# Low halves of the projections' weights and their sums of squares on VectorE instead of GpSimd

## The chip, the core and the metric

The program runs on one core of one Trainium2 chip. A core has five engines that work side by side, each from its own list, in order: TensorE (PE in the profile; its weight loads are PEld), VectorE (DVE), ScalarE (ACT), GpSimd (POOL) and SyncE (SP), which here issues nearly all DMA transfers. An instruction starts when it is at the head of its engine's list and the semaphores that it waits for are set. The metric is the time of one execution on the device in microseconds; the figure for a kernel is the median of its runs.

## The reference

Two layers over 1024 latent tokens and 256 context tokens of width 1024, in float32. Cut to what matters here:

```python
for l in range(2):
    mod = silu(c) @ w_mod[l] + b_mod[l]          # six shifts, scales and gates; the same for c_ctx
    h = rmsnorm(x, g_norm1[l]) * (1 + sc1) + sh1  # the same for the context
    pf, mq, mk, mv, mo, mg, cq, ckv, kr = split(h @ w_in[l])
    y_f = real(fft2(pf))
    q, k = silu(conv5([mq, mk]))                  # depthwise, 5 taps
    y_m = mlstm_both_directions(q, k, mv, gates(mg)) * sigmoid(mo)
    y_a = attention(rmsnorm(cq) @ w_uq, rmsnorm(ckv) @ w_ukv, kr)
    x = x + ga1 * (concat(y_f, y_m, y_a) @ w_out[l])
    x = x + ga2 * (square(relu(modulate(rmsnorm(x, g_norm2[l])) @ w_up[l])) @ w_down[l])
return rmsnorm(x, g_final)
```

## The kernel before

**Numbers in two halves.** TensorE multiplies float32r operands. To keep the accuracy of float32, `split` writes every operand as a high half (ScalarE, a copy in float32r, line 147) and a low half (source minus high half, line 148), and `mm3` forms a product from three matmuls: high by high, high by low, low by high (lines 138, 143, 144 among others). `split` gives the low half to GpSimd where its caller names no engine.

**Tiles.** Tokens go in three blocks (`BLK`): two of 512 latent tokens and one of 256 context tokens. Features lie on the partitions, 128 at a time, so one elementwise instruction is mostly 128x512.

**Weights of the projections.** `wunit` fetches a piece of 128x512 (SyncE, line 167) into `wf`, a ring of three buffers, and splits it into `wr`, a ring of ten. `unit` calls it four times for one unit of the input projection; the output projection calls it too, through `wtile`. The first two units of layer 0 land in parts of the input's own buffers instead of `wf` (`wr<-x` in the profile), and some at the start of layer 1 in `r`. The low half stands on VectorE for the odd ones of the first eight calls, on GpSimd for all others. `wq` and `wkv`, the weights of the attention's second projections, are fetched and split in the same manner beside the gates' arithmetic (line 644).

**Norms.** A sum of squares over the features is collected tile by tile: ScalarE squares, a second engine adds (`accum_ss`, line 267, for the low-rank norms and the output projection; lines 348 to 351 at the start; `put`, line 1426, at the end of the MLP, which stays as it is). `rstd_bcast` sums over the partitions on TensorE, computes the inverse root by three Newton rounds, on GpSimd (lines 180 to 183) or VectorE (185 to 187), and spreads it by TensorE again (line 201). At the start, block 0 takes the GpSimd form, and GpSimd then multiplies the eight tiles by it (line 359). The low-rank norms take the GpSimd form in layer 1 only (`LNE`).

**Modulation.** `modulate` (blocks 1 and 2 in layer 0) writes the halves of eight tiles; for odd `k` through `split`. `mod0` (block 0) has its own choice of engines and stays.

**Around the convolution.** For each of six tiles of mq and mk, TensorE projects, ScalarE copies into `rb` (line 673), VectorE does five taps (675, 677), ScalarE a tanh, VectorE the closing product (679). Between these rows VectorE does the products of weights and `c` that give the modulation of later stages (line 235, weight tiles `gt` and `wf` fetched by SyncE at line 232), the norms, and the mLSTM gates (lines 580 to 635), whose vectors take a turn through DRAM (lines 593 to 599: `dA` and `dB` out, `A` and `B` back).

**What sets the order.** The code is written stage by stage with priorities. The tile framework then sets each engine's list by an estimated timeline of the whole program, so that an instruction given to another engine also changes the order of rows around it, on all engines. The lists themselves are fixed when the program runs.

Of the kernel before, what the change touches and what calls it, by code (L numbers as in the profile page):

```python
# [9 lines left out]
ALU = mybir.AluOpType  # L10
# [53 lines left out]
def build(tc, A, out, dbg=None):  # L64
# [9 lines left out]
    def T(pool, shape, dt=F32, tag=None, **kw):  # L74
        if tag in alias:
            tag, kw = alias[tag], {}
            if isinstance(tag, tuple):
                pool, tag = tag
        assert kw == seen.setdefault((id(pool), tag), kw) or not kw, tag
        kw = seen[(id(pool), tag)]  # L80
        return pool.tile(list(shape), dt, tag=tag, name=nm(tag), **kw)
# [24 lines left out]
    V, S, G, PE = nc.vector, nc.scalar, nc.gpsimd, nc.tensor  # L106

    def f32(ap):
        return ap.bitcast(F32)
# [36 lines left out]
    def split(dst, src, hi=None, lo=None):  # L146
        (hi or S).activation(dst[0], src, AF.Copy) if (hi is None or hi is S) else hi.tensor_copy(dst[0], src)  # L147
        (lo or G).tensor_tensor(dst[1], src, f32(dst[0]), ALU.subtract)  # L148
# [11 lines left out]

    NRING = 10

    wcnt = [0, 9]

    def wunit(src, f=None):
        f = T(ring, [128, 512], tag="wf", bufs=3) if f is None else f
        nc.sync.dma_start(f, src)
        r = T(ring, [128, 2, 512], F32R, tag="wr", bufs=NRING)
        wcnt[0] += 1
        split((r[:, 0], r[:, 1]), f, lo=V if wcnt[0] < wcnt[1] and wcnt[0] % 2 else G)  # L170
        return r

    def rstd_small(y, v, n, pool, rows=128, eng=None):
# [87 lines left out]
    def accum_ss(ss, x, j, pool, n, eng=None):  # L261
        if j == 0:
            S.activation(ss[:, :n], x, AF.Square)
        else:
            sq = T(pool, [128, 512], tag="sq")
            S.activation(sq[:, :n], x, AF.Square)
            (eng or G).tensor_tensor(ss[:, :n], ss[:, :n], sq[:, :n], ALU.add)

    def modulate(l, i, b, xt, ss, h, pool, psp, tag):
        n, w = BLK[b][1], BLK[b][2]  # L270
        R = rstd_bcast(ss, n, D, pool, psp, tag)
        for k in range(8):
            t = T(pool, [128, 512], tag="md_t")[:, :n]
            V.scalar_tensor_tensor(t, xt[:, k, :], Gm[l][i][:, w, k:k + 1], R[:, :n], ALU.mult, ALU.mult)
            sh = modT[l][:, w, 24 * i + k:24 * i + k + 1]
            if k % 2 == 0:
                S.activation(h[:, 0, k, :], t, AF.Identity, bias=sh)
                V.scalar_tensor_tensor(h[:, 1, k, :], t, sh, f32(h[:, 0, k, :]), ALU.add, ALU.subtract)
            else:
                S.activation(t, t, AF.Identity, bias=sh)  # L280
                split((h[:, 0, k, :], h[:, 1, k, :]), t)

    big = {}

# [33 lines left out]
    ss = [T(xp, [128, BLK[b][1]], tag=f"ss{b}") for b in range(3)]  # L318
# [18 lines left out]
    def load_x(b):  # L337
        t0, n, _ = BLK[b]
        if b:
            S.copy(xT[b][:, :, 0:1], modT[0][:, 0, XJ[b - 1]:XJ[b - 1] + 1].unsqueeze(1).to_broadcast([128, 8, 1]))  # L340
        for q in range(4):
            nc.sync.dma_start(xT[b][:, 2 * q:2 * q + 2], A["x"][:, 2 * q:2 * q + 2, t0:t0 + n])
        c = [ss[b], a2[:, 2560:3072]] if b == 0 else [ss[b]]
        for k in range(8):
            if k >= len(c):
                sq = T(wk, [128, 512], tag="sq")
            dst = sq if k >= len(c) else c[k]
            S.activation(dst[:, :n], xT[b][:, k], AF.Square)
            if k >= len(c):
                p = k % len(c)  # L350
                (V, G)[p].tensor_tensor(c[p][:, :n], c[p][:, :n], sq[:, :n], ALU.add)
        if b == 0:
            V.tensor_tensor(ss[b], ss[b], c[1], ALU.add)
        if b == 0:
            R = rstd_bcast(ss[b], n, D, wk, pst, "t", eng=G)
            Rs = T(wk, [128, 512], tag="gw")
            S.copy(Rs, R)
            for k in range(8):
                G.tensor_tensor(xT[b][:, k], xT[b][:, k], Rs, ALU.mult)
# [68 lines left out]
    for l in range(2):  # L428
# [81 lines left out]
        r = unit_(False)  # L510
        r1 = unit_(False)
        for b in range(3):
            t0, n, w = BLK[b]
# [29 lines left out]
        r = unit_()  # L543
        r1 = unit_(False)
        for b in range(3):
            t0, n, w = BLK[b]
# [92 lines left out]
        for w_, src, n0 in ((wq, A["w_uq"][l], 1024), (wkv, A["w_ukv"][l], 640)):  # L639
            for c0 in range(0, n0, 512):  # L640
                c1 = min(n0, c0 + 512)
                f = T(ring, [128, 512], tag="wf", bufs=3)
                nc.sync.dma_start(f[:, :c1 - c0], src[:, c0:c1])
                split((w_[:, 0, c0:c1], w_[:, 1, c0:c1]), f[:, :c1 - c0])


        cvh = vec[:, V_CV + 30 * l:V_CV + 30 * l + 30]
        for n_, ti in enumerate((4, 5, 2, 3, 0, 1)):
            rate = GR[2 + n_ // 2]
            if ti % 2 == 0:  # L650
                r = unit_()
# [17 lines left out]
            for b in range(3 if cx else 2):  # L669
                t0, n, w = BLK[b]  # L670
# [3 lines left out]
                c0, c1 = ((0, 510), (510, 1024), (1026, 1282))[b]  # L674
# [8 lines left out]
        r = unit_()  # L683
# [358 lines left out]
        xT, ss, yT, wo = [None] * 3, [None] * 3, [None] * 3, []  # L1042
# [453 lines left out]
        for c in range(NCH):  # L1496
# [66 lines left out]
            if lastc and last:  # L1563
# [5 lines left out]
                for th in range(2):  # L1569
# [4 lines left out]
                    for j in range(4):  # L1574
                        xj, sq = xT[1][:, j, tl], u2[j][:, tl]
# [126 lines left out]
```

## Time and profile before

| | |
|---|---|
| median of 3 runs | 3015.47 us (3014.15 to 3018.77) |
| the profiled execution | 3019.14 us |
| its span, first to last instruction | 3017.3 us |
| its granted TensorE clock, mean | 0.962 |
| HBM read, written | 283.74 MB, 90.02 MB |

A row of instructions reads: line, engine, operation, out<-in, shapes, count | busy us, mean ns of one | idle time of the engine ahead of them and what ended it. A row of a timeline begins with the start and the duration in us, and has the idle time ahead of it, with what ended it, in square brackets; "x3" there are three instructions in one row, one behind another. In a row of waits stand the engine, the instruction that waited <- what it waited for, the us in total, the times, and the longest. The span of the program in us: start and modulation 0 to 165, the rest of layer 0's input projection with the convolution to about 330, then mLSTM and attention, output projection with the second norm about 650 to 870, MLP to about 1660, and the same for layer 1 from there, with the input projection to 1930 and the output projection about 2190 to 2350.

### The profile page before, as it was taken

Reading aid. Unit: us, or ns where it says so; the run is one execution under the profiler, and the core shown is the slowest. Engines: PE = TensorE matmul, PEld = TensorE weight load, DVE = VectorE, ACT = ScalarE, POOL = GpSimd, SP = SyncE. Lnnn points to the kernel's source line nnn. Section 1 sums busy time; section 2 is a strip of 40 time slices with the busy share of each in tenths; the row PEclk is TensorE's granted clock in tenths of the full one; section 3 lists DMA queues with packets and bytes.
Section 4 is the critical chain, followed back from the end, with each engine's and each line's share of the span. In section 5 each row is a group of like instructions: output and inputs, shape, how many; then the busy total and the mean of one; then the engine's idle time right before and its main releaser. Section 6 shows DMA issues by size and latency. Waiting matters only on the chain.

```text
span 3017.3 us, 40556 instructions
## 1 busy us (share of the span) xinstructions
PE 2827.9 (94%) x14320; PEld 2334.7 (77%) x14320; DVE 2128.6 (71%) x4170; ACT 1178.6 (39%) x2283; POOL 517.3 (17%) x517
## 2 busy tenths in 40 slices
PE   7988989989989999999999898899999999989996
PEld 6877867757878888888887787867767788868885
DVE  8769668742498898786787527468633976678887
ACT  3322245443353333243245432245433534334444
POOL 4213100011200000021125133100022000013334
PEclk7999999999999999999999999899999999999998
DMA  6514575323355544633121212455134443253321
GB/s 237 161 55 128 146 174 156 110 91 120 109 175 175 168 171 165 240 112 116 45 91 56 88 42 85 124 147 147 56 120 139 146 134 115 105 198 99 105 85 56
DMA packets 277871, 376.44 MB, mean 125 GB/s; under 512 B 63396, under 2 KB 154468, under 8 KB 276004
## 3 DMA queue, kind: packets, MB, share of 16 engines
q1 hardware_dynamic: 274788, 366.51, 39.0%
q0 software_dynamic: 576, 4.20, 0.4%
q10 hardware_dynamic: 2304, 3.15, 0.3%
q8 instruction: 113, 1.85, 0.3%
q14 instruction: 90, 0.74, 0.1%
HBM read 283.74 MB, written 90.02 MB: 124 GB/s over the span
## 4 chain that ended last, share of the span: by engine, by line
PE 59%; DVE 18%; DMA 10%; issue 6%; POOL 2%; ACT 2%; SPq 0%; DVEq 0%; POOLq 0%; ACTq 0%
PE mm L138 9%; PE mm L143 7%; PE mm L144 7%; PE v L1141 4%; PE mm L135 4%; PE mm L136 4%; PE mm L134 4%; DVE junk L235 3%; DVE A L148 2%; DVE ac L677 2%; PE mm L1466 2%; PE mm L140 2%; PE mm L141 2%; DMA wf<-in_w_mt 2%; PE t L1466 2%
## 5 line engine op out<-in xcount | busy, mean ns | idle before, releaser
L138 PE MATMUL mm<-A,wr 128*128 128x512 f32 (+1 forms) x840 | 312.9, 375 | 24.6 <-ACT rb L673 12.3
L135 PE MATMUL mm<-A 128*128 128x512 f32 (+1 forms) x654 | 251.3, 389 | 11.2 <-DVE A L148 8.9
L134 PE MATMUL mm<-A 128*128 128x512 f32 (+1 forms) x654 | 238.1, 387 | 5.6 <-ACT A L147 4.4
L136 PE MATMUL mm<-A 128*128 128x512 f32 (+1 forms) x654 | 242.9, 387 | 0.3 <-DVE A L148 0.3
L138 PEld LDWEIGHTS mm<-A,wr 128*128 128x128 f32 x840 | 161.2, 193 | 54.0 <-ACT rb L673 14.0
L143 PE MATMUL mm<-A,wr 128*128 128x512 f32 (+1 forms) x520 | 193.0, 372 | 6.2 <-DVE A L148 4.2
L144 PE MATMUL mm<-A,wr 128*128 128x512 f32 (+1 forms) x520 | 191.6, 369 | 0.0
L1141 PE MATMUL v<-PT,Vt 128*97 128x512 f32 (+1 forms) x336 | 172.8, 599 | 16.6 <-ACT PT L1140 16.1
L138 PE MATMUL mm<-A,c 128*128 128x512 f32 (+1 forms) x520 | 184.0, 355 | 4.5 <-ACT A L147 3.4
L143 PE MATMUL mm<-A,c 128*128 128x512 f32 (+1 forms) x520 | 184.3, 355 | 2.7 <-DVE A L148 2.6
L144 PE MATMUL mm<-A,c 128*128 128x512 f32 (+1 forms) x520 | 182.5, 353 | 1.3 <-DVE c L148 1.3
L148 POOL TENSOR_TENSOR wr<-wf,wr 128x512 fp32r<-128x512 f32 x88 | 123.7, 1413 | 292.1 <-ACT wr L147 230.3
L147 ACT ACTIVATE A<-wr 128x512 fp32r<-128x512 f32 x188 | 114.2, 625 | 147.9 <-PE mm L135 59.2
L147 ACT ACTIVATE A<-A 128x512 fp32r<-128x512 f32 x174 | 106.9, 625 | 160.0 <-PE mm L135 86.6
L148 DVE TENSOR_TENSOR A<-wr,A 128x512 fp32r<-128x512 f32 x146 | 128.7, 893 | 43.4 <-ACT A L147 29.0
L235 DVE SCALAR_TENSOR_TENSOR junk<-wf,t 128x512 bf16<-128x512 f32 x192 | 130.8, 681 | 33.7 <-DMA wf<-in_w_mt 32.0
L135 PEld LDWEIGHTS mm<-A 128*128 128x128 f32 x654 | 123.9, 190 | 39.4 <-DVE A L148 11.7
L1140 ACT ACTIVATE PT<-s 128x512 f32<-128x512 f32 (+1 forms) x168 | 97.0, 583 | 138.6 <-PE s L144 138.0
L134 PEld LDWEIGHTS mm<-A 128*128 128x128 f32 x654 | 123.1, 189 | 31.2 <-ACT A L147 6.8
L136 PEld LDWEIGHTS mm<-A 128*128 128x128 f32 x654 | 123.5, 189 | 25.0 <-DVE A L148 0.7
L138 PE MATMUL mm<-wr,A 128*128 128x256 f32 x464 | 133.4, 288 | 6.6 <-ACT rb L673 4.7
L143 PE MATMUL mm<-wr,A 128*128 128x256 f32 x464 | 133.1, 288 | 0.0
(497 smaller groups left out, 7802.9 us busy)
## 6 DMA issues: line engine op xcount, KB each, us to landing
wf<-in_w_mt SPq DMA_DIRECT2D x96, 256.0 KB
x<-in_w_up SPq DMA_DIRECT2D x40, 512.0 KB
r<-in_w_up SPq DMA_DIRECT2D x38, 512.0 KB
wr<-in_w_dn SPq DMA_DIRECT2D x36, 512.0 KB
gt<-in_w_mt SPq DMA_DIRECT2D x64, 256.0 KB
da<-wf SPq DMA_DIRECT2D x64, 256.0 KB
da<-p SPq DMA_DIRECT2D x64, 256.0 KB
wf<-in_w_in SPq DMA_DIRECT2D x56, 256.0 KB
```

Of the source, the lines that this page charges most:

```text
L134: PE.matmul(ps, lh, rh, start=first, stop=False, skip_group_check=True)
L135: PE.matmul(ps, lh, rl, start=False, stop=False, skip_group_check=True)
L136: PE.matmul(ps, ll, rh, start=False, stop=last, skip_group_check=True)
L138: PE.matmul(ps, lh, rh, start=first, stop=False)
L143: PE.matmul(ps, lh, rl, start=False, stop=False)
L144: PE.matmul(ps, ll, rh, start=False, stop=last)
L147: (hi or S).activation(dst[0], src, AF.Copy) if (hi is None or hi is S) else hi.tensor_copy(dst[0], src)
L148: (lo or G).tensor_tensor(dst[1], src, f32(dst[0]), ALU.subtract)
L235: V.scalar_tensor_tensor(junk, f, 1.0, cb[w], ALU.mult, ALU.mult, accum_out=(ga, modT[l])[kh][:, w, j:j + 1])
L1140: S.activation(PT[:, :nq], ps[:, :nq], AF.Exp, scale=scale)
L1141: PE.matmul(po[:97, :nq], Vt[kt // 2][:, kt % 2, h % 2], PT[:, :nq], start=i == 0, stop=i == len(kts) - 1)
L1466: PE.matmul(o, blk[f"B{h + 1}{q + 1}"][k][:, 128 * jj:128 * jj + 128], f[:, k, 256 * h:256 * h + 256], start=h + k == 0, stop=h * k == 3)
```

## The change

Five places give work to VectorE (`V`) that GpSimd (`G`) had; what is computed stays.

```diff
@@ wunit: the low half of every weight piece
-    wcnt = [0, 9]
+    wcnt = [0]
-        split((r[:, 0], r[:, 1]), f, lo=V if wcnt[0] < wcnt[1] and wcnt[0] % 2 else G)
+        split((r[:, 0], r[:, 1]), f, lo=V)
@@ accum_ss
-            (eng or G).tensor_tensor(ss[:, :n], ss[:, :n], sq[:, :n], ALU.add)
+            V.tensor_tensor(ss[:, :n], ss[:, :n], sq[:, :n], ALU.add)
@@ modulate, odd k
-                split((h[:, 0, k, :], h[:, 1, k, :]), t)
+                split((h[:, 0, k, :], h[:, 1, k, :]), t, lo=V)
@@ load_x
-                (V, G)[p].tensor_tensor(c[p][:, :n], c[p][:, :n], sq[:, :n], ALU.add)
+                V.tensor_tensor(c[p][:, :n], c[p][:, :n], sq[:, :n], ALU.add)
@@ wq, wkv
-                split((w_[:, 0, c0:c1], w_[:, 1, c0:c1]), f[:, :c1 - c0])
+                split((w_[:, 0, c0:c1], w_[:, 1, c0:c1]), f[:, :c1 - c0], lo=V)
```

159 instructions change their engine: 100 splits of `wr`, 8 of `wq` and `wkv`, 8 of the modulation, 40 adds of line 267 and 3 of line 351. GpSimd keeps the Newton rounds, line 359, line 1426, its share of the splits of activations in MLP and attention, and the clearing of buffers.

**First place: GpSimd's list at the start, the norm of block 0.** `rs_t` and `rb_y` are the Newton rounds of lines 180 to 183, `wr` the weights. Before:

```order
10 L180 TENSOR_TENSOR rs_t_201<-rb_y_197 128x4
11 L148 TENSOR_TENSOR wr_265<-x_40_116,wr_265 128x512
12 L181 TENSOR_TENSOR rs_t_201<-rs_t_201,rs_h_198 128x4
13 L148 TENSOR_TENSOR wr_273<-x_40_116,wr_273 128x512
14 L182 TENSOR_SCALAR rs_t_201<-rs_t_201 128x4
15 L183 TENSOR_TENSOR rb_y_197<-rb_y_197,rs_t_201 128x4
```

Of the change:

```order
7 L180 TENSOR_TENSOR rs_t_201<-rb_y_197 128x4
8 L181 TENSOR_TENSOR rs_t_201<-rs_t_201,rs_h_198 128x4
9 L182 TENSOR_SCALAR rs_t_201<-rs_t_201 128x4
10 L183 TENSOR_TENSOR rb_y_197<-rb_y_197,rs_t_201 128x4
11 L180 TENSOR_TENSOR rs_t_201<-rb_y_197 128x4
```

The two splits between the steps of the first round are gone, and so are the adds of line 351 that stood ahead of it; two more rounds and line 359 follow with nothing between.

**Second place: VectorE's list in the convolution of layer 0.** `ac` is the convolution (675, 677), `cm` and `ma` the gates, `rs_h` and `rb_y` a low-rank norm, `junk` line 235. Before:

```order
286 L677 SCALAR_TENSOR_TENSOR ac_1949<-rb_1945,vec_62,ac_1949 128x510
287 L175 TENSOR_SCALAR rs_h_1777<-rb_v_1774 128x2
288 L677 SCALAR_TENSOR_TENSOR ac_1949<-rb_1945,vec_62,ac_1949 128x510
289 L603 SCALAR_TENSOR_TENSOR ma_1870<-A_356_1864,B_357_1865 4x2
290 L235 SCALAR_TENSOR_TENSOR junk_2042,mod_6_66<-gt_2040,gv_1996 128x512
291 L489 SCALAR_TENSOR_TENSOR ev_1687<-ev_1687,vec_62,t_1690 128x256
292 L176 TENSOR_SCALAR rb_y_1776<-rb_v_1774 128x2
```

Of the change:

```order
319 L677 SCALAR_TENSOR_TENSOR ac_1949<-rb_1945,vec_62,ac_1949 128x510
320 L175 TENSOR_SCALAR rs_h_1777<-rb_v_1774 128x2
321 L235 SCALAR_TENSOR_TENSOR junk_2042,mod_6_66<-gt_2040,gv_1996 128x512
322 L148 TENSOR_TENSOR wr_1932<-wf_1930,wr_1932 128x512
323 L677 SCALAR_TENSOR_TENSOR ac_1949<-rb_1945,vec_62,ac_1949 128x510
324 L489 SCALAR_TENSOR_TENSOR ev_1687<-ev_1687,vec_62,t_1690 128x256
325 L176 TENSOR_SCALAR rb_y_1776<-rb_v_1774 128x2
326 L603 SCALAR_TENSOR_TENSOR ma_1870<-A_356_1864,B_357_1865 4x2
```

The split of `wr_1932` now stands ahead of the second tap and of line 489; line 603, the gates' return from DRAM, stands later.

**Third place: SyncE's list for the same weight** (`wf_1930`, what `wr_1932` is split from; `dA`, `dB`, `A`, `B` are the gates' turn through DRAM). Before:

```order
97 L594 DMA dB_85<-bt_1850 40x1 x2
98 L593 DMA dA_84<-cm_1852 40x1 x2
99 L599 DMA B_357_1865<-dB_85 4x10
100 L598 DMA A_356_1864<-dA_84 4x10 x2
101 L599 DMA B_357_1865<-dB_85 4x10
102 L167 DMA wf_1930<-in_w_in 128x512
```

Of the change:

```order
97 L167 DMA wf_1925<-in_w_in 128x512
98 L167 DMA wf_1930<-in_w_in 128x512
99 L594 DMA dB_85<-bt_1850 40x1 x2
100 L593 DMA dA_84<-cm_1852 40x1 x2
101 L599 DMA B_357_1865<-dB_85 4x10
```

The fetch has moved from behind the gates' turn to ahead of it.

## The prediction

> **What bounds the kernel now.** I read the page's busy times, its slices and its chain first, then windows by stage and what PE waits for in them, then the rows of POOL and VectorE.
>
> ```profile
> PE 2827.9 (94%) x14320; PEld 2334.7 (77%) x14320; DVE 2128.6 (71%) x4170; ACT 1178.6 (39%) x2283; POOL 517.3 (17%) x517
> PE   7988989989989999999999898899999999989996
> DVE  8769668742498898786787527468633976678887
> PE 59%; DVE 18%; DMA 10%; issue 6%; POOL 2%; ACT 2%; SPq 0%; DVEq 0%; POOLq 0%; ACTq 0%
> ```
>
> PE is busy in 94% of the span, so at most 3017.3 − 2827.9 = 189 us are open to any change that leaves PE's work alone, as this one does. The chain gives DVE 18% and POOL 2%. Each slice is 75 us: PE stands at 8 or 9 in nearly all, DVE swings between 2 and 9, so which of them ends a wait must be asked stage by stage. I cut the span at the stages that the change touches:
>
> ```profile
> 0.00:60.00 60.00, 42.78 (x207) 39.84 (x208) 45.75 (x78) 19.44 (x36) 32.83 (x33) 0.70 0.74 277
> 60.00:200.00 140.00, 129.35 (x775) 114.89 (x775) 95.87 (x293) 51.17 (x101) 30.01 (x29) 0.96 0.36 110
> 200.00:330.00 130.00, 114.20 (x677) 100.97 (x676) 114.59 (x259) 34.62 (x78) 29.98 (x35) 0.96 0.40 125
> 650.00:870.00 220.00, 198.56 (x993) 161.21 (x993) 105.36 (x204) 88.92 (x167) 45.32 (x37) 0.93 0.39 122
> 1600.00:1700.00 100.00, 85.07 (x382) 70.01 (x381) 77.49 (x133) 50.78 (x99) 43.64 (x31) 0.93 0.21 80
> 1750.00:1930.00 180.00, 171.76 (x1042) 153.95 (x1041) 87.06 (x153) 51.34 (x113) 53.58 (x107) 0.99 0.20 61
> 2190.00:2350.00 160.00, 151.50 (x630) 114.88 (x630) 61.19 (x110) 59.80 (x103) 39.13 (x30) 0.96 0.42 133
> ```
>
> The busy columns are PE, weight loads, DVE, ACT, POOL. From 200 to 330, the convolution of layer 0, DVE is busy 114.6 of 130 us and PE idles 15.8: here DVE leads. In the two output projections (650 to 870, 2190 to 2350) DVE is below half. The start and the boundary of the layers (1600 to 1700) lie between.
>
> **What moves, and what one instruction costs.** 159 instructions leave POOL.
>
> ```profile
> L148 POOL TENSOR_TENSOR wr<-wf,wr 128x512 fp32r<-128x512 f32 x88 | 123.7, 1413 | 292.1 <-ACT wr L147 230.3 <-DMA wf<-in_w_out 52.3 <-DMA gt<-in_w_mt 9.3
> L267 POOL TENSOR_TENSOR ss<-ss,p 128x512 f32<-128x512 f32 x20 | 27.5, 1375 | 75.7 <-ACT p L266 75.7
> L148 DVE TENSOR_TENSOR wr<-x,wr 128x512 fp32r<-128x512 f32 x24 | 15.6, 685 | 0.0
> ```
>
> On POOL a split costs 1.41 us and a sum 1.38; on DVE the same split, which the kernel has there for other weights (wr<-x), is 0.685, or 0.60 back to back, as the next fence shows. Taken at 0.60 for 512 columns, 159 are about 95 us of DVE work (a few are narrower), 3% of the span. What they give back is that DVE is held while POOL works:
>
> ```profile
> 295.65 1.81 DVE L677 SCALAR_TENSOR_TENSOR ac<-rb,vec,ac 128x514 f32<-128x514 f32 x3
> 297.98 3.89 DVE L677 SCALAR_TENSOR_TENSOR ac<-rb,vec,ac 128x514 f32<-128x514 f32 x3
> 298.28 3.04 POOL L148 TENSOR_TENSOR wr<-wf,wr 128x512 fp32r<-128x512 f32 x2 [9.29 <-DMA gt<-in_w_mt]
> ```
>
> Three convolution steps take 1.81 us (0.60 each) with POOL quiet and 3.89 beside two POOL splits. So a POOL split costs a running DVE 2.08/2 = 1.04 us, and on DVE itself 0.60: **0.44 us are won** for each, where DVE never rests. Where DVE rests, nothing is won by this and nothing lost.
>
> The Trainium skill (Perfetto Trace Analysis, Optimizing Scalar/DVE Operations) warns that GpSimd and DVE share an SBUF read port, so that moving operations between those two might not help. The first half agrees with the 3.89 us above; by the second the sum below would be 0, and this is the rival "wash".
>
> **Stage by stage.** Each term is the change in the span, with its ends in brackets.
>
> *Convolution of layer 0, 200 to 330.* 18 instructions move (16 of wr, 2 of wq), 18 × 0.60 = 10.8 us onto DVE.
>
> ```profile
> L677 DVE SCALAR_TENSOR_TENSOR ac<-rb,vec,ac 128x510 f32<-128x510 f32 x24 | 21.1, 879 | 0.0
> L677 DVE SCALAR_TENSOR_TENSOR ac<-rb,vec,ac 128x514 f32<-128x514 f32 x24 | 19.8, 823 | 0.0
> L677 DVE SCALAR_TENSOR_TENSOR ac<-rb,vec,ac 128x256 f32<-128x256 f32 x24 | 13.5, 562 | 0.0
> L679 DVE SCALAR_TENSOR_TENSOR ac<-rb,ac 128x510 f32<-128x510 f32 x6 | 5.2, 861 | 0.0
> L679 DVE SCALAR_TENSOR_TENSOR ac<-rb,ac 128x256 f32<-128x256 f32 x6 | 4.1, 690 | 0.0
> PE mm L138 <- ACT rb L673: 11.0, 3, 7.0
> ```
>
> I estimate the undisturbed time at 0.68 for 510 and 514 columns (the split's) and, with half the columns, at 0.42. The excess of L677 is then 24 × (0.199 + 0.143 + 0.142) = 11.6 us, that of L679 6 × (0.181 + 0.270) = 2.7. So 14.3 us go and 10.8 come: DVE −3.5. PE's 11.0 us on L673 (the copy into `rb`, whose buffer comes free when DVE's chain is done) says that PE follows DVE there, but DVE also waits for transfers, so I take **−2.5** [−3.5 to +8.9, the latter under the rivals].
>
> *Startup, 0 to 60.* 9 move, three of them adds of L351.
>
> ```profile
> 18.76 0.57 POOL L180 TENSOR_TENSOR rs_t<-rb_y 128x4 f32<-128x4 f32 x1 [5.74 <-DVE rb_y L176]
> 19.29 1.85 POOL L148 TENSOR_TENSOR wr<-x,wr 128x512 fp32r<-128x512 f32 x1
> 21.25 2.27 POOL L148 TENSOR_TENSOR wr<-x,wr 128x512 fp32r<-128x512 f32 x1
> 23.47 1.22 POOL L182 TENSOR_SCALAR rs_t<-rs_t 128x4 f32<-128x4 f32 x1
> PE t L201 <- POOL rb_y L183: 6.3, 1, 6.3
> ```
>
> The chain of the first norm (L180 to L183, three rounds on POOL) has two splits in it, 1.85 + 2.27 = 4.1 us, and PE waits 6.3 for its end. The listing of the change above shows them gone from it. Against it, six splits on DVE are 3.6 us, and small steps of POOL stay slow while DVE runs two-input work (1.22 us for a 128x4 row). I take half, **−2** [−4.1 to +1.5].
>
> *60 to 200.* 24 move (8 of the modulation, 13 weights, 3 sums), 14.4 us at most on a DVE that rests 140 − 95.9 = 44.
>
> ```profile
> PE t L201 <- DVE rb_y L187: 6.9, 2, 6.6
> PE mm L143 <- POOL A L148: 0.9, 1, 0.9
> ```
>
> The 0.9 goes; the 6.9 hangs on a norm chain on DVE that now has splits ahead of it, each of which can wait for its weight. I take **0** [−3 to +3, half of the 6.6 either way].
>
> *Output projections, 650 to 870 and 2190 to 2350.* 37 and 30 move, 40 us of DVE work in 115 and 99 us of rest: hidden. In each norm the last sum (L267) ends 1.38 − 0.69 = 0.7 us sooner, three blocks in two layers, and not all on the path: **−1** [−2 to 0]. Without that rest it would cost up to 0.60 each.
>
> *Boundary, 1600 to 1700.* 10 splits move.
>
> ```profile
> 1652.87 1.83 POOL L1426 TENSOR_TENSOR ss<-ss,wf 128x512 f32<-128x512 f32 x1
> 1654.67 1.74 POOL L148 TENSOR_TENSOR wr<-r,wr 128x512 fp32r<-128x512 f32 x1
> PE t L194 <- POOL ss L1426: 3.4, 1, 3.4
> ```
>
> POOL's sums L1426 stay, and PE waits 3.4 for the last. One split of 1.74 among them is shown, so about half the wait goes: **−1.5** [−3.4 to +1, as DVE is busy 77% here and gets 6 us].
>
> *Input projection of layer 1, 1700 to 1930.* 8 and 22 move.
>
> ```profile
> PE mm L138 <- ACT rb L673: 6.0, 2, 4.7
> PE t L201 <- POOL rb_y L183: 2.2, 1, 2.2
> ```
>
> DVE rests 93 us of 180, PE only 8.2. Part of the 2.2 goes with the splits in front of it: **−0.5** [−3 to +3].
>
> Sum: −2.5 − 2 + 0 − 1 − 1.5 − 0.5 = **−7.5 us**. The profiled execution took 3019.1 (span 3017.3 and 1.8 around it), which becomes 3011.6; it lies 3.7 above the median of the three runs, so on the median's footing 3015.5 − 7.5 = **3008.0**.
>
> **The rivals.** *Slower: DVE's queue stands at a weight that has not landed.* On POOL a late split held only other splits; on DVE it holds the convolution, the norms and the gates.
>
> ```profile
> 212.52 1.98 POOL L148 TENSOR_TENSOR wr<-wf,wr 128x512 fp32r<-128x512 f32 x1 [11.49 <-ACT wr L147]
> 210.13 0.46 DVE L489 SCALAR_TENSOR_TENSOR ev<-ev,vec,t 128x256 f32<-128x256 f32 x1
> 217.81 0.14 DVE L186 TENSOR_TENSOR rs_t<-rs_t,rs_h 128x2 f32<-128x2 f32 x1
> 226.85 1.29 POOL L148 TENSOR_TENSOR wr<-wf,wr 128x512 fp32r<-128x512 f32 x1 [7.07 <-ACT wr L147]
> 1832.05 2.72 POOL L148 TENSOR_TENSOR wr<-wf,wr 128x512 fp32r<-128x512 f32 x2 [5.50 <-ACT wr L147]
> ```
>
> The first of these (wr_1932) is ready at 212.5 and now stands ahead of L489, which ran at 210.1: 2.4 us. The next but one stands behind L186, which ended at 217.95, and was ready at 226.85: 8.9, which takes in the first. In layer 1 a split that POOL waited 5.5 for goes the same way. If weights land as before and PE follows, 8.9 + 5.5 = +14.4 on the −7.5 gives 3015.5 + 6.9 = **3022.4**. It decides as soon as a weight lands more than a few us behind its place in DVE's order. Against it: SyncE now issues that weight ahead of the gate vectors' transfers, not behind them (listing of the change), and the later split of POOL no longer delays the buffer's return.
>
> *Wash.* DVE pays 0.60 for work and gets 0.60 back, or the PE waits that end sooner reappear behind transfers: DMA has 10% of the chain. 0 gives **3015.5**. For it speaks that the waits of PE that name POOL in the rows above are only 6.3 + 0.9 + 3.4 + 2.2 = 12.8 us in all.
>
> *All of it counts.* Those 12.8 us go whole, and the convolution gives its 3.5: −16.3, **2999.2**. Against it: POOL's own chains remain, and what comes next (DVE, ACT) is seldom more than a few us behind.
>
> *It doesn't do what it says.* The order of each engine is set anew, so places far from the edits move; the MLP and attention stages show PE full, and there I see nothing to lose.
>
> **How the numbers follow.** About 0.2%, 6 us, can be told from no change, so faster is below 3009.4 and slower above 3021.5. The forecast (−13 to −2, that is 3002.5 to 3013.5) has 0.42, of it 0.30 faster and 0.12 same; all of it counts 0.14, faster; wash 0.23, of it 0.01 faster, 0.20 same and 0.02 slower, as the new order may cost or win a few us anywhere; slow queue 0.21, of it 0.18 slower and 0.03 same. Together **faster 0.45, same 0.35, slower 0.20**. The sum of the low ends of the terms is −3.5 − 4.1 − 3 − 2 − 3.4 − 3 = −19.0, 2996.5; the slow rival's 3022.4 with the upper ends of the startup (+1.5 in place of −2) reaches 3025.9. The range is **2996 to 3026**.
>
> **What would show it right or wrong.** L677 at about 0.68 in place of 0.88 from 200 to 330, with POOL nearly empty there; POOL's L180 to L183 without a gap at 19, and PE's wait for L183 below 4.5 us; PE's wait for L1426 below 2. It is wrong if DVE shows idle time from 200 to 330, or in layer 1's convolution, that is ended by ACT's L147 on `wr` (the queue standing at a weight), or if PE's wait for `rb` L673 is not below 11.0 and 6.0; or if the gain lies in stages that the edits don't touch, where only the new order can have made it.

## The result, and the profile after

The changed kernel is faster by 0.85%, more than three times what was forecast, and outside the range.

| | |
|---|---|
| the changed kernel, median of 4 runs | 2990.55 us (2984.1 to 2996.41) |
| the kernel before, beside it, 4 runs | 3017.12 us (3014.15 to 3018.78) |
| ratio | 0.9915, 95% interval 0.9894 to 0.9935 |
| profiled execution, span | 2996.41 us, 2994.6 us |

Single executions of one kernel scatter by some 10 us here (those of the kernel before lay between 3004 and 3028 in all comparisons). Times of experiments are therefore ratios against the kernel before on the same chip, with 95% intervals; in us they are given for 3017. A single trace shows where, not how much to the last us.

The page of the changed kernel, busy times, three rows of slices and the chain:

```profile
PE 2827.2 (94%) x14320; PEld 2335.4 (78%) x14320; DVE 2174.0 (73%) x4329; ACT 1179.8 (39%) x2283; POOL 301.9 (10%) x358
PE   7998999999989999999999999899999999989996
DVE  7779668753598888786787537368645976678887
POOL 3000100000000000021124020100000000023334
PE 67%; DVE 14%; DMA 9%; issue 6%; POOL 2%; ACT 2%; SPq 0%; DVEq 0%; POOLq 0%; ACTq 0%
```

DVE took 159 instructions and became only 45.4 us busier (2174.0 against 2128.6), though at the 0.69 us that a 128x512 row takes they are some 100 us: most of the rest came back from instructions of its own that no longer stood beside POOL (line 677 alone by 13 us). Its share of the chain fell from 18% to 14%. The stages, at bounds that cover about the same work:

```profile
0.00:60.00 60.00, 43.56 (x205) 40.74 (x206) 44.35 (x87) 18.48 (x33) 20.76 (x24) 0.66 0.80 296
60.00:200.00 140.00, 131.97 (x778) 117.36 (x777) 102.12 (x314) 52.19 (x103) 2.90 (x5) 0.94 0.32 102
200.00:325.00 125.00, 116.89 (x682) 103.46 (x681) 113.04 (x285) 34.60 (x78) 3.06 (x17) 0.95 0.43 135
200.00:324.40 124.40, 116.29 (x677) 102.86 (x676) 112.47 (x283) 34.60 (x78) 3.06 (x17) 0.95 0.43 134
```

The last row holds the same 677 matmuls as the prediction's row from 200 to 330: DVE works 2.1 us less and rests 3.5 us less, and the granted clock is no higher (0.95 against 0.96). Its waits for a weight tile of line 235, before (200 to 330) and after (200 to 325), and what TensorE still waits for `rb` after:

```profile
DVE junk L235 <- DMA gt<-in_w_mt: 8.9, 6, 1.9
```

```profile
DVE junk L235 <- DMA gt<-in_w_mt: 3.5, 3, 1.8
PE mm L138 <- ACT rb L673: 5.3, 2, 3.4
```

For the next table every TensorE instruction was looked up in both traces (the n-th of its line and shape, where both have as many), and the difference of the starts was averaged (median) in bins of 50 us. The differences of these bins give each stage's step. The second trace of the changed kernel is from the run changed_again below.

| stage (us of before) | forecast | first trace | second trace |
|---|---|---|---|
| to 150 | −2 and 0 | −0.1 | −5.0 |
| convolution of layer 0, to 300 | −2.5 | −5.6 | −6.0 |
| mLSTM and attention, to 600 | 0 | +2.2 | −2.3 |
| end of attention and output projection, to 700 | −0.5 | −8.9 | −10.2 |
| rest of layer 0, to 1600 | 0 | +1.9 | −0.5 |
| boundary, to 1700 | −1.5 | −3.8 | −4.3 |
| input projection of layer 1, to 1950 | −0.5 | −5.5 | −6.9 |
| attention and output projection of layer 1, to 2200 | −0.5 | −4.0 | −3.6 |

Five steps repeat in both traces. Two of them stand where they were expected, only larger; the largest was priced at half a microsecond (−1 for both layers' output projections). The last one can't be put down to the pieces that moved: −3 of the first trace's −4 falls between 2120 and 2140, while the first output projection piece of layer 1 stands at 2199. There the granted clock of the kernel before was low in its trace, and that of the changed kernel wasn't:

```profile
2120.00:2130.00 10.00, 8.86 (x40) 7.62 (x40) 6.61 (x18) 4.34 (x12) 0.00 (x0) 0.66 0.26 74
```

```profile
2100.00:2110.00 10.00, 8.92 (x62) 7.79 (x63) 9.07 (x30) 5.74 (x14) 0.00 (x0) 1.00 0.27 73
```

The run out_only below, whose lists on TensorE and ScalarE are those of the kernel before up to 2200, has the same −3.2 there. From 2180 to 2350, where layer 1's pieces stand, the two traces have −0.7 and −1.1. Elsewhere, too, a step of one trace alone can be off by 5 us (first row).

### The profile page after: what moved, and what is told of

Read it like the earlier page. It is cut to its first block, busy times and chain, and to the rows that moved or that the text cites. A ratio compares the mean times of both kernels' runs of the same rounds, so it can differ in the third digit from the quotient of the medians.

```text
span 2994.6 us, 40430 instructions
## 1 busy us (share of the span) xinstructions
PE 2827.2 (94%) x14320; PEld 2335.4 (78%) x14320; DVE 2174.0 (73%) x4329; ACT 1179.8 (39%) x2283; POOL 301.9 (10%) x358
## 4 chain that ended last, share of the span: by engine, by line
PE 67%; DVE 14%; DMA 9%; issue 6%; POOL 2%; ACT 2%; SPq 0%; DVEq 0%; POOLq 0%; ACTq 0%
PE mm L138 11%; PE mm L143 9%; PE mm L144 9%; PE v L1141 4%; PE mm L135 4%; PE mm L136 4%; PE mm L134 4%; DVE junk L235 2%; PE mm L140 2%; PE mm L141 2%; PE mm L1466 2%; DMA wf<-in_w_mt 2%; PE t L1466 2%; DVE A L148 2%; POOL A L148 1%
## 5 line engine op out<-in xcount | busy, mean ns | idle before, releaser
L138 PE MATMUL mm<-A,wr 128*128 128x512 f32 (+1 forms) x840 | 316.6, 379 | 19.9 <-DVE x L1420 6.9
L143 PE MATMUL mm<-A,wr 128*128 128x512 f32 (+1 forms) x520 | 196.7, 379 | 5.0 <-DVE A L148 3.2
L144 PE MATMUL mm<-A,wr 128*128 128x512 f32 (+1 forms) x520 | 195.1, 376 | 0.0
L148 DVE TENSOR_TENSOR A<-wr,A 128x512 fp32r<-128x512 f32 x146 | 126.1, 875 | 41.6 <-ACT A L147 28.4
L1140 ACT ACTIVATE PT<-s 128x512 f32<-128x512 f32 (+1 forms) x168 | 97.0, 583 | 129.0 <-PE s L144 128.5
L148 DVE TENSOR_TENSOR A<-A,A 128x512 fp32r<-128x512 f32 x131 | 116.0, 894 | 23.5 <-ACT A L147 22.6
L143 PE MATMUL mm<-wr,A 128*128 128x256 f32 x464 | 132.2, 286 | 0.0
```

The lines of the kernel that those rows point to most:

```text
L138: PE.matmul(ps, lh, rh, start=first, stop=False)
L143: PE.matmul(ps, lh, rl, start=False, stop=False)
L144: PE.matmul(ps, ll, rh, start=False, stop=last)
L1140: S.activation(PT[:, :nq], ps[:, :nq], AF.Exp, scale=scale)
```

## The experiments

Fourteen kernels ran beside the kernel before. Their expectations weigh three explanations: "port", that VectorE is held while GpSimd works; "order", that the newly set lists make the difference; and "ring", that a weight's buffer comes free late. The first three runs move one part of the change alone.

**out_only**: the kernel before, with the output projections' pieces alone moved.

```diff
-    def wunit(src, f=None):
+    def wunit(src, f=None, lo=None):
-        split((r[:, 0], r[:, 1]), f, lo=V if wcnt[0] < wcnt[1] and wcnt[0] % 2 else G)
+        split((r[:, 0], r[:, 1]), f, lo=lo or (V if wcnt[0] < wcnt[1] and wcnt[0] % 2 else G))
@@ wtile
-            return [wunit(src[:, 512 * q:512 * q + 512]).rearrange("p l (k m) -> p l k m", k=4) for q in range(2)]
+            return [wunit(src[:, 512 * q:512 * q + 512], lo=V).rearrange("p l (k m) -> p l k m", k=4) for q in range(2)]
```

> Kernel before, with only the output projections' weight pieces (32 of the 100) split on VectorE; all else as before. Ring theory (a piece's low half on GpSimd keeps its wf buffer, so the fetch three pieces on starts late, ScalarE stands in its list at a weight that has not landed, the exponentials behind it come late, TensorE waits and its granted clock falls): 8 to 13 us faster than before, about 3006; TensorE's wait for PT L1140 at 630 to 680 falls from 8.0 to below 4 us, and the clock of 0.50 at 670 to 680 goes. Port theory (only VectorE's time beside GpSimd counts, as in the prediction): VectorE rests there, so 0 to 2 us. Order theory (the gain is luck of the newly set order): any size, and the waits named need not change.

Measured: 0.9967 (0.9954 to 0.998), −10 us; in its trace −10.3 between 600 and 700 and −0.6 from 2180 to 2350 (the −3.2 at 2120 is the one spoken of above). The pieces that the prediction called hidden carry more than a third of the gain, and it comes in layer 0. The waits of TensorE (us in total, times, longest) at the end of layer 0's attention, in the kernel before and in out_only:

```profile
PE v L1141 <- ACT PT L1140: 8.0, 6, 3.5
```

```profile
PE v L1141 <- ACT PT L1140: 3.8, 6, 0.7
```

**in_only**: only the input projection's pieces, wq and wkv.

```diff
+        split((r[:, 0], r[:, 1]), f, lo=lo or V)
@@ wtile
+            return [wunit(src[:, 512 * q:512 * q + 512], lo=G).rearrange("p l (k m) -> p l k m", k=4) for q in range(2)]
@@ wq, wkv
+                split((w_[:, 0, c0:c1], w_[:, 1, c0:c1]), f[:, :c1 - c0], lo=V)
```

> Kernel before, with only the input projections' weight pieces and wq, wkv split on VectorE (76 instructions); output projections' pieces, sums, modulation and line 351 as before. Port theory and ring theory alike: the convolution stages give 5.5 us each as in the changed kernel, with about 4 at the boundary of the layers: 9 to 15 us faster, about 3005. Told apart inside: by the port theory L677 falls to about 0.75 us and TensorE's wait for rb L673 to about half; by the ring theory the wait of VectorE for gt in L235 falls too. Order theory: not the sum of the parts.

Measured: 0.9948 (0.9928 to 0.9967), −16 us, the upper edge. In the trace −5.3 in layer 0's convolution, −1.5 at the boundary, −5.8 in layer 1's input projection, but also −6.7 between 300 and 600, where none of its instructions stands. In the convolution both signs came: L677 fell to 0.75 us, and the wait for `gt` from 8.9 to 4.6 us; TensorE's wait for `rb` fell from 11.0 to 7.0, less than to half.

**sums_only**: the other three edits.

```diff
@@ accum_ss, modulate, load_x
+            V.tensor_tensor(ss[:, :n], ss[:, :n], sq[:, :n], ALU.add)
+                split((h[:, 0, k, :], h[:, 1, k, :]), t, lo=V)
+                V.tensor_tensor(c[p][:, :n], c[p][:, :n], sq[:, :n], ALU.add)
```

> Kernel before, with only the sums of line 267, the modulation's odd low halves and line 351 on VectorE (51 instructions); all weights as before. The changed kernel was 1 to 1.5 us later than before at 60 us, and the sums' places show little: -2 to +2 us by every theory but the order theory, which lets it be off by 5 either way.

Measured: 0.9976 (0.9963 to 0.9989), −7 us: wrong. Its trace has −7.5 us between 300 and 600 and nothing of size elsewhere but −4 before 150. No edit lies in 300 to 600, yet between 330 and 640 another matmul stands at 1317 of 1755 places of TensorE's list. The waits in that stage, of the kernel before (330 to 640) and of sums_only (327 to 628):

```profile
PE v L1141 <- ACT PT L1140: 5.1, 8, 1.1
PE m L1003 <- ACT Q L147: 4.3, 3, 2.1
```

```profile
PE v L1141 <- ACT PT L1140: 3.3, 6, 0.9
PE m L1003 <- ACT Q L147: 1.8, 1, 1.8
```

Four runs have this very order of matmuls there: sums_only, in_only, weights_all and weights_rest. Their traces gain 5.3 to 7.8 us between 300 and 600; those of the runs with the kernel before's order there lie between −2.3 and +4.3. So the newly set order is worth some 6 us in that stage. The parts add up to −33 us, the whole change gave −26: the whole change keeps the order of the kernel before in that stage. In the convolution the wait for `gt` falls here too (4.7 us), with every weight split still on GpSimd, so new lists can bring that fall without a split that moves; the stage gains nothing by it here (+0.4), as L677 takes 0.88 to 0.89 us with 510 and 514 columns.

**ring4**: engines as before, `wf` with four buffers from the output projection on.

```diff
+    def wfb(nb):
+        return {} if (id(ring), "wf") in seen else dict(bufs=nb)
-    def wunit(src, f=None):
+    def wunit(src, f=None, nb=3):
-        f = T(ring, [128, 512], tag="wf", bufs=3) if f is None else f
+        f = T(ring, [128, 512], tag="wf", **wfb(nb)) if f is None else f
@@ wtile
-            return [wunit(src[:, 512 * q:512 * q + 512]).rearrange("p l (k m) -> p l k m", k=4) for q in range(2)]
+            return [wunit(src[:, 512 * q:512 * q + 512], nb=4).rearrange("p l (k m) -> p l k m", k=4) for q in range(2)]
```

> Kernel before, all engines as before, but from the output projection of layer 0 on the weights' ring wf has four buffers in place of three. Ring theory: a fetch no longer waits for GpSimd's split three pieces back, so most of the 8 us at 650 to 690 and of the 4 us at 2130 to 2220 come without any work moved: 5 to 12 us faster than before, and TensorE's wait for PT L1140 at 630 to 680 below 5 us in place of 8.0. Port theory: nothing leaves GpSimd, so 0, within 2 us.

Measured: 1.0012 (0.9997 to 1.0026), and TensorE's wait for PT is 7.1 us, its longest 4.5. The ring theory falls as stated. SyncE's own waits show why, kernel before and ring4 (L167 is L170 there, L1057 is L1060):

```profile
SPq L167 <- POOL wr L148: 10.0, 9, 2.0
SPq L1057 <- DMA q<-dy: 3.9, 2, 2.1
SPq L1057 <- DVE A L148: 1.2, 2, 0.9
```

```profile
SPq L1060 <- DVE A L148: 6.4, 5, 2.0
SPq L1060 <- DMA q<-dy: 5.2, 4, 2.0
SPq L170 <- POOL wr L148: 4.4, 5, 1.8
```

The weights wait less (4.4 in place of 10.0), and the fetches of `q`, next in the same list, wait more. What TensorE waited for was another thing. ScalarE's timeline of the kernel before at that place:

```profile
666.79 0.58 ACT L1140 ACTIVATE PT<-s 128x512 f32<-128x512 f32 x1
667.60 0.63 ACT L147 ACTIVATE A<-q 128x512 fp32r<-128x512 f32 x1 [0.23 <-DMA q<-dy]
668.25 0.58 ACT L147 ACTIVATE Q<-m 1x512 fp32r<-1x512 f32 x1
671.92 0.42 ACT L147 ACTIVATE A<-q 128x256 fp32r<-128x256 f32 x1 [3.08 <-DMA q<-dy]
672.25 0.58 ACT L1140 ACTIVATE PT<-s 128x512 f32<-128x512 f32 x1
```

The exponential at 672.25 stands in the list behind a copy of `q` that waits 3.08 us for its transfer, and TensorE waits 3.5 for the exponential. In the changed kernel (and in out_only) the list has the exponential first:

```profile
662.31 0.63 ACT L147 ACTIVATE wr<-wf 128x512 fp32r<-128x512 f32 x1 [2.01 <-DMA wf<-in_w_out]
662.84 0.58 ACT L1140 ACTIVATE PT<-s 128x512 f32<-128x512 f32 x1
```

**exp_first** tests this: the kernel before with that place of ScalarE's list set by hand.

```diff
+                hk["PT", bi] = S.activation(PT[:, :nq], ps[:, :nq], AF.Exp, scale=scale)
@@ load_y
+                with behind(("PT", len(blocks) - 3) if not l and (b or k == 0) else None):
+                    split((yT[b][:, 0, k], yT[b][:, 1, k]), yf[:, :n], lo=V)
```

> Kernel before, all engines and TensorE's order as before; in layer 0 ScalarE's high halves of y for block 2 and the last tile of block 0 are held in the list behind the exponential that ended last in the attention's block before the last but one, as they stand in the changed kernel. Order theory (the 8 to 10 us at 670 to 690 come from ScalarE's exponential PT no longer standing behind a copy of q that waits for its transfer): 6 to 10 us faster than before, TensorE's wait for PT L1140 at 630 to 680 from 8.0 to below 5 us, and the clock of 0.50 there gone. If GpSimd's time on the splits is what counts: 0 to 2 us.

Measured: 0.9985 (0.9973 to 0.9998), −4.5 us, between its two forecasts, with the wait for PT at 5.9 us; −5.9 between 600 and 700 in its trace. TensorE's list is that of the kernel before, and VectorE's differs in eight places, as the low halves follow. So about half of what out_only wins in layer 0 is order, though the interval leaves anything from 0.6 to 8 us. The price of the wait is more than its length, as the clock shows. The windows of the kernel before at 650, 660 and 670, and that of exp_first at 670 (columns as above, the clock in the third place from the end):

```profile
650.00:660.00 10.00, 9.30 (x37) 6.76 (x38) 7.60 (x13) 6.74 (x13) 7.68 (x6) 1.00 0.72 227
660.00:670.00 10.00, 7.46 (x30) 4.55 (x28) 5.05 (x9) 4.90 (x9) 5.11 (x4) 0.95 0.58 176
670.00:680.00 10.00, 7.09 (x23) 5.46 (x24) 1.03 (x3) 2.86 (x7) 0.00 (x0) 0.50 0.26 80
```

```profile
670.00:680.00 10.00, 8.23 (x45) 5.88 (x45) 2.90 (x7) 4.56 (x10) 0.00 (x0) 1.00 0.46 131
```

The same 27 matmuls behind the wait start within 7.8 us in the kernel before (672.88 to 680.68) and within 4.5 us in exp_first (670.44 to 674.93): a wait of 3.5 us cost another 3.3 us behind it.

**exp_first_ring4**: both at once.

> Kernel before, all splits where they were, with both ScalarE's order as in run exp_first and the four buffers of run ring4. If the output projection's 10 us are order and turn of the ring together: 8 to 10 us faster than before. If GpSimd's hold on VectorE and the length of its splits are the rest: no more than run exp_first, 3 to 6 us, or less.

Measured: 0.9972 (0.996 to 0.9985), −8 us, at the lower end of the first forecast; but the interval meets that of exp_first, and between 600 and 700 its trace has −5.5 beside −5.9. That a longer ring helps once the order is right isn't shown.

**port_load** asks what POOL's instructions cost when nothing waits for them. It is the changed kernel with

```diff
         split((r[:, 0], r[:, 1]), f, lo=V)
+        if 8 < wcnt[0] <= 36:
+            G.tensor_tensor(T(cst, [128, 512], mybir.dt.bfloat16, tag="jp"), f32(r[:, 0]), f32(r[:, 1]), ALU.add)
```

> The changed kernel, with 28 added GpSimd instructions of two inputs (128x512), one behind each of the input projection's weight splits of layer 0 that are not in the first eight; they read wr and write a tile that nobody reads, so no engine waits for them and the lists of the other engines stay as they are. Port theory: in 200 to 325 L677 goes from a mean of 0.75 us back to 0.85 or more, TensorE waits longer for rb L673, and the time is 4 to 7 us longer than that of the changed kernel. Order theory: no change beyond 2 us.

Measured: 0.994 (0.9922 to 0.9959) against 0.9915: 7 to 8 us of the gain gone, though the intervals overlap. The traces tell it more surely: this one loses 10.7 us between 200 and 300 and gets 2.4 back behind it, where the two traces of the changed kernel differ by 0.5. DVE from 200 to 325, the changed kernel first, then port_load (L677 is L679 there):

```profile
L677 DVE SCALAR_TENSOR_TENSOR ac<-rb,vec,ac 128x514 f32<-128x514 f32 x24 | 17.9, 747 | 0.0
L677 DVE SCALAR_TENSOR_TENSOR ac<-rb,vec,ac 128x256 f32<-128x256 f32 x24 | 11.5, 478 | 0.0
L148 DVE TENSOR_TENSOR wr<-wf,wr 128x512 fp32r<-128x512 f32 x16 | 10.9, 685 | 2.1 <-ACT wr L147 2.1
```

```profile
L679 DVE SCALAR_TENSOR_TENSOR ac<-rb,vec,ac 128x514 f32<-128x514 f32 x24 | 18.6, 774 | 0.0
L148 DVE TENSOR_TENSOR wr<-wf,wr 128x512 fp32r<-128x512 f32 x16 | 13.8, 865 | 1.3 <-ACT wr L147 1.3
L679 DVE SCALAR_TENSOR_TENSOR ac<-rb,vec,ac 128x256 f32<-128x256 f32 x24 | 13.7, 569 | 0.0
```

```profile
PE mm L138 <- ACT rb L675: 14.2, 3, 7.0
```

TensorE's wait for `rb` is back from 5.3 to 14.2 us. The lists of TensorE, ScalarE and VectorE are unchanged and no one waits for the added instructions, yet the 282 instructions of VectorE that ran from 200 to 324.4 in the changed kernel, one by one the same, take 143.7 us in place of 132.2 (durations added up). So sixteen POOL instructions cost VectorE 11.5/16 = 0.72 us each, and TensorE 10.7/16 = 0.67. One sign missed: L677 with 510 and 514 columns rose only to 0.77, not to 0.85; the splits (0.69 to 0.87) and the narrow rows took the hold.

**port_load_out** does the same in the output projections (32 instructions).

```diff
-    def wunit(src, f=None):
+    def wunit(src, f=None, po=False):
+        if po:
+            G.tensor_tensor(T(cst, [128, 512], mybir.dt.bfloat16, tag="jp"), f32(r[:, 0]), f32(r[:, 1]), ALU.add)
@@ wtile
+            return [wunit(src[:, 512 * q:512 * q + 512], po=True).rearrange("p l (k m) -> p l k m", k=4) for q in range(2)]
```

> The changed kernel, with one added GpSimd instruction of two inputs (128x512) behind each of the 32 weight splits of the output projections, reading wr and writing a tile that nobody reads; the lists of the other engines stay as they are. Order theory for that stage (the 10 us there come from ScalarE's exponential no longer behind a copy of q): 0 to 2 us slower than the changed kernel, the clock at 656 to 676 stays 1.00. Port theory: 4 us or more slower, and the wait for PT L1140 comes back.

Measured: 0.9949 (0.9933 to 0.9964) against 0.9916 for the changed kernel beside it: 10 us lost. In the trace +5.5 between 650 and 750 and +6.7 at 2200, against that of changed_again. Of DVE from 640 to 660 in changed_again, then in port_load_out:

```profile
L148 DVE TENSOR_TENSOR wr<-wf,wr 128x512 fp32r<-128x512 f32 x7 | 4.8, 688 | 1.3 <-ACT wr L147 1.3
L1004 DVE TENSOR_REDUCE mx<-m 128x1 f32<-128x512 f32 x6 | 4.1, 689 | 0.1
```

```profile
L148 DVE TENSOR_TENSOR wr<-wf,wr 128x512 fp32r<-128x512 f32 x7 | 7.5, 1078 | 0.0
L1006 DVE TENSOR_REDUCE mx<-m 128x1 f32<-128x512 f32 x7 | 4.7, 678 | 0.0
```

The order theory had put 0 to 2 us on this, so a hold of DVE costs time there. But the port theory's second sign failed: the wait for PT L1140 doesn't come back (2.3 us beside 3.2), and the clock stays at 1.00 from 650 to 680. And the run prices the hold on a DVE that has the splits as well. The window of the changed kernel that matches 650 to 660 has DVE at 9.93 of 10 us, where the kernel before, in the row above, had 7.60:

```profile
646.50:656.50 10.00, 8.73 (x33) 5.76 (x33) 9.93 (x18) 6.95 (x14) 0.00 (x0) 1.00 0.73 228
```

In the kernel before, the rows of DVE that POOL held from 645 to 668 are five splits of `q` and `qf` (0.85 and 0.99 us in place of 0.68), about 1.1 us in all. So port_load_out doesn't show what the splits had cost there on GpSimd.

**in_layer1** and **in_layer1_wq**: the kernel before with only layer 1's input projection pieces moved, and then with layer 1's wq and wkv too.

```diff
@@ unit, handed on to split by wunit
+                      lo=V if l else None
@@ wq, wkv, in in_layer1_wq only
+                split((w_[:, 0, c0:c1], w_[:, 1, c0:c1]), f[:, :c1 - c0], lo=V if l else None)
```

> Kernel before, with only layer 1's input projection weight pieces (36) split on VectorE; nothing ahead of the end of layer 0's MLP changes. Port theory: boundary and convolution of layer 1 as in the changed kernel, 2 to 4 and 5 to 7 us less: 7 to 11 us faster than before. As the prediction priced it (boundary and input projection of layer 1 together): 2 us faster.

> The kernel of run in_layer1 (layer 1's 36 input projection pieces on VectorE), with layer 1's four splits of wq and wkv on VectorE too. If these are what separates run in_layer1 (its convolution stage gave nothing in the trace) from the changed kernel (5.5 us there): 4 to 6 us faster than run in_layer1, 8 to 10 faster than before, and TensorE's wait for rb L673 in 1800 to 1900 gone. If not, within 2 us of run in_layer1.

Measured: 0.9986 (0.9975 to 0.9998), −4 us, less than the port theory's 7 to 11, and 0.9965 (0.9953 to 0.9976), −10.5 us, as its expectation had it. The first has its gain at the boundary (−3.6) and none in the convolution; there TensorE still waits 5.3 us for `rb`. With four more instructions off POOL that wait is gone from the stage's list, and the trace has −3.5 and −6.2. So the stage's gain hangs on the last few POOL splits beside the convolution, in this kernel. By which way isn't shown: in in_layer1 L677 with 510 columns is already at 0.74 us, but SyncE's fetches wait there for a split of `wq`:

```profile
SPq L167 <- POOL wq L148: 8.1, 2, 6.9
```

and in wq_back below, which gives these splits back to the changed kernel, the stage still gains 3.1 us.

**changed_again** is the changed kernel itself. The other three start from it: **wq_back** gives `wq` and `wkv` back to GpSimd (8 splits, not the 12 that its expectation counts), **weights_all** lines 267 and 351, and **weights_rest** is weights_all with two more moves off GpSimd.

```diff
@@ wq_back
+                split((w_[:, 0, c0:c1], w_[:, 1, c0:c1]), f[:, :c1 - c0])
@@ weights_all, weights_rest
+            (eng or G).tensor_tensor(ss[:, :n], ss[:, :n], sq[:, :n], ALU.add)
+                (V, G)[p].tensor_tensor(c[p][:, :n], c[p][:, :n], sq[:, :n], ALU.add)
@@ weights_rest
+LNE = (0, 0)
+                    V.tensor_tensor(ss[b], ss[b], sq, ALU.add)
```

> The changed kernel itself once more, timed beside the kernel before and the three runs below on the same chip, with a second trace. By every theory 22 to 29 us faster than before, and the stages' steps of its first trace come again: 200 to 330 by 4 to 7 us, the end of layer 0's attention by 7 to 10, layer 1's boundary and convolution by 8 to 10.

> The changed kernel with the 12 splits of wq and wkv given back to GpSimd. TensorE's list is the same to about 200 us and differs in 4 rows in the convolution, but it differs in over 400 rows in the attention of layer 0, where no instruction changes engine. Port theory: 1 to 3 us slower (two of them stand in each convolution). Order theory: the attention stage moves by several us, of either sign.

> The changed kernel with line 351's adds and the sums of line 267 given back to GpSimd: weights, wq, wkv and modulation on VectorE. The attention of layer 0 gets the order that it has in the run with only the input projection moved, though none of its instructions changes engine. Order theory: that stage, 325 to 635, is some 8 us shorter than in the changed kernel, so 2980 to 2986 in all, though 43 instructions fewer are moved. Port theory: a little slower than the changed kernel, 0 to 4 us.

> The run with weights and modulation on VectorE and the sums of lines 267 and 351 on GpSimd, and besides line 1426's sums and layer 1's low-rank norms on VectorE in place of GpSimd. The boundary's wait for ss L1426 goes: 0 to 4 us faster than that run, 2982 to 2988.

| run | ratio | 95% interval |
|---|---|---|
| changed_again | 0.9916 | 0.9899 to 0.9934 |
| wq_back | 0.9927 | 0.9906 to 0.9949 |
| weights_all | 0.9898 | 0.9883 to 0.9913 |
| weights_rest | 0.9881 | 0.9863 to 0.99 |

changed_again repeats the gain. wq_back is no different from the changed kernel within its interval, though over 400 rows of the attention's order are: not every new order matters. weights_all moves 43 instructions fewer and comes out about 5 us faster than the changed kernel, but the intervals overlap; its trace gains 5.3 us between 300 and 600, with the order of sums_only and in_only. **weights_rest is the fastest**: 2974.0 us beside 2984.2 of the changed kernel and 3008.1 of the kernel before on that chip, 10 us ahead of the change and below its forecast of 2982 to 2988. By the traces, part of that lead is the attention's order, which it shares with weights_all. Its two further moves take POOL out of the boundary's sums and of layer 1's norms. How much each of the two brings wasn't tried.

## Why the prediction was wrong

- **What bounds the kernel: right.** TensorE stayed at 2827 us of work, and all of the gain came out of its idle time.
- **The price of a POOL instruction beside a busy DVE: right mechanism, clean time misread.** The row of three convolution steps at 1.81 us mixes three shapes (514, 256 and 510 columns, at 0.75, 0.48 and 0.75 us each, with overlaps), so its 0.60 is the time of none. The estimates of 0.68 and 0.42, taken from other rows, were too low: in the changed kernel, where POOL is nearly empty, L677 takes 0.747 and 0.478. Its excess was then 7.1 us and not 11.6; that of L679 was 2.7, as forecast. The 1.04 us per split held for those two rows, but port_load has 0.72 on average, hardly more than the 0.69 that a split takes on DVE.
- **Convolution, −2.5: the work right, the waits left out.** DVE's work fell by 2.1 and 2.6 us in the two traces, as the −2.5 said, but the stage gave −5.6 and −6.0: DVE's rest fell by some 3.5 as well, mostly its wait for `gt` (8.9 to 3.5 us). The prediction had held DVE's waits for transfers as they were. sums_only points to the new lists for this fall, and shows none of its worth while the splits still hold DVE.
- **"Output projections: hidden. −1": the step that failed.** It set 37 and 30 instructions against DVE's rest in windows of 220 and 160 us. In layer 0, 10 of the 16 pieces stand between 645 and 668, at the end of the attention, where DVE is at 76% before and 99% after, and where a late row of ScalarE's list makes TensorE wait. The prediction put nothing on TensorE's wait of 8.0 us for PT there, as it doesn't name POOL. out_only puts 10 us on the stage in place of 1. Of these, exp_first got 4.5 by the order of ScalarE's list, with every split on POOL. What the rest is stays open: the hold that the kernel before shows there is about 1.1 us, and port_load_out prices a hold in the changed kernel, not in this one. In layer 1 "hidden" was right: the same burst of ten pieces, from 2199 to 2216, gives about 1 us.
- **Input projection of layer 1, −0.5: failed.** The prediction printed TensorE's wait of 6.0 us for `rb` and priced only the one of 2.2 beside it, as DVE rested half of the window. The wait for `rb` is what went (to nothing in both traces of the changed kernel; steps −5.5 and −6.9), the other one rose to 3.3. in_layer1_wq shows the same gain by this stage's pieces, `wq` and `wkv` alone.
- **Boundary, −1.5: right, too small.** The wait for L1426 went from 3.4 us to nothing, the step is −3.8.
- **Startup, −2: not confirmed.** The two splits are gone from the norm's chain, yet it starts 1.3 us later, and its first steps are slower. POOL's timeline after:

```profile
20.09 2.31 POOL L180 TENSOR_TENSOR rs_t<-rb_y 128x4 f32<-128x4 f32 x1 [19.64 <-DVE rb_y L176]
22.48 1.19 POOL L181 TENSOR_TENSOR rs_t<-rs_t,rs_h 128x4 f32<-128x4 f32 x1
```

  It begins at 20.09 in place of 18.76, and a 128x4 row takes 2.31 us beside a DVE without a rest, as much as the longer of the two splits. From its start to the end of line 183's last row the chain took 11.2 us before and 9.4 after. TensorE's wait fell only from 6.3 to 5.0, and the two traces of the changed kernel disagree on this stage (−0.1 and −5.0).
- **The rival "slower": didn't come.** DVE's waits for a piece's high half between 200 and 325 are 2.1 us, in its L148 row above: not nothing, as the prediction's sign had it, but far from its 8.9. That the earlier fetches met the weights is likely, not tested.
- **"All of it counts", at 2999: the nearest rival, still short**, as it added up only the waits that name POOL. Most of the gain lay in waits that name ScalarE: `rb`, whose copy follows DVE's chain, and PT, whose place in ScalarE's list the new order set.

The Trainium skill (SBUF — State Buffer, Who interferes with whom) has it that a VectorE instruction with two SBUF inputs contends with a GpSimd instruction that reads SBUF, and that one with at most one SBUF input, outside the two-port modes, doesn't. The traces agree: 688 to 1078 ns for the split, 689 to 678 for L1004, whose one input is in PSUM. The Trainium skill's sentence weighed in the prediction (Perfetto Trace Analysis, Optimizing Scalar/DVE Operations), that moving work between the two might not help, was read there as a sum of 0; here out_only, in_only and in_layer1_wq all gain.

## What to carry to other kernels

An instruction on GpSimd isn't free just because GpSimd is idle. If it reads SBUF beside a VectorE that runs two-input work, count its cost on VectorE before its cost on its own engine: here 0.3 us (10 us for 32, port_load_out) to 1.0 us (the prediction's two rows) for one of 1.4 us. Look for a full engine in windows as short as the burst of work that moves, not in the stage: a VectorE that was busy 48% of 220 us was at 76% and then 99% in the 10 us that mattered. Price every long wait of the engine that bounds the kernel in such a window, also one that names a third engine. And where a scheduler sets the order anew, part of any result is the new order: test a part with the order held, by a load that nobody waits for or by one place set by hand.

## What the runs showed of the hardware

- A long wait of TensorE can be followed by a slower clock: behind waits of 1.9 and 3.5 us the granted clock fell from 1.00 to 0.50 from 670 to 680, and the same 27 matmuls took 7.8 us in place of 4.5. The Trainium skill (TensorE: Matmul & The Clock Gate, Why this matters for your kernels) names idle gaps of about 3 us as what halves the rate; the 3.5 us wait fits. The kernel before's clock of 0.66 from 2120 to 2130 came without any such wait (the longest from 2090 to 2150 was 0.7 us).
- Reducing instructions of VectorE with one input, in PSUM, were untouched by GpSimd (689 and 678 ns); those with two inputs in SBUF rise by half (688 to 1078 ns for the split) in the same 20 us.
- GpSimd's smallest instructions suffer as well: a 128x4 row took 2.31 us beside a VectorE without a rest, and 0.20 us some 8 us later in the same chain, when VectorE stood still.
